# A mixture-of-experts stage whose places of 96 and 64 slots stand in another sequence

## Chip, cores and metric

One NeuronCore of a Trainium2 chip. The metric is the device time of one execution in microseconds (us). The kernel before was timed in three runs: 1676.42 us median, 1673.38 to 1678.52.

## What is computed

Two layers of an encoder over 256 tokens of width 1024, in float32. Layer 0 mixes by a recurrence and a state space model, then attends to a memory, then goes through a dense feed-forward. Layer 1 mixes by differential attention, attends to the memory, and ends in eight experts of which each token takes two. The change touches the experts alone:

```python
top_logits, top_idx = lax.top_k(logits, TOP_K)
top_w = jax.nn.softmax(top_logits, axis=-1)
gates = jnp.sum(jax.nn.one_hot(top_idx, N_EXPERTS, dtype=F32) * top_w[..., None], axis=-2)
out = jnp.zeros(h.shape, F32)
for e in range(N_EXPERTS):
    y_e = swiglu(h, w_gate[e], w_up[e], w_down[e]).astype(F32)
    out = out + gates[..., e:e + 1] * y_e
```

An expert's hidden width is 3584, so its three matrices hold 3 x 1024 x 3584 floats, 44.04 MB, and all eight 352 MB.

## The kernel before, in words

The stage of the experts is a loop over eight *places*, `r` = 0 to 7 (the last loop of the kernel, under `manual_schedule`, so TensorE's order is the order of the code). A place handles one expert, and only the tokens that chose it: these are gathered into a fixed number of slots, 96 or 64. `NG[r]` says how many groups of 32 slots place `r` has, 3 or 2; in the kernel before it is (3, 3, 2, 3, 2, 3, 3, 2). Place 0 always holds expert 0. The other seven experts are sorted by their number of tokens on the chip (`order`, L1730 on), and the table `by_size` in `_constants` hands the four with most tokens to the places of 96 and the three others to the places of 64; `caps` (L1755 to L1757) gives the capacities by that same rank, and a branch behind the loop takes up tokens that did not fit. In this data nothing overflows: the branch's body is not in the trace.

In a place, TensorE goes through four steps `i` = 0 to 3, each for two slices of 512 hidden columns (the last for two of 256):

- `up(r, i)` (L1860, its matmuls are recorded at the helper's line L195 as `pgu<-raw,gx`): the gathered tokens `gx` are the stationary operand, 32 columns at a time, the weights `raw` the moving one. Four matmuls of 32 columns lie beside each other in the array. The step has two halves of four row blocks; a half needs four pieces of weights (gate and up, of two slices), all four almost from its start.
- `hidden` and `turned` (ScalarE, VectorE, and transposes `ptA` and, with 96 slots only, `ptC`): the activation, turned for the next matmul.
- `down(r, i)` (`pd<-raw,th`), which runs one step late, behind the next `up`: four pieces of weights, the last step two.

Once a place, at fixed points of this order: `scatter` (`psc`) of the place before, twelve matmuls for 96 slots and eight for 64; `prepare(r + 1)` (`ptp`), which makes the next place's scatter matrix; and, in places 0, 2, 4 and 6 behind their last `up`, `gather` (`pgt`) for the next set of places. The sets are fixed: (0), (1, 2), (3, 4), (5, 6), (7). A gather computes as many columns for each of its places as the widest of the set has, 32 matmuls in any case.

Weights come by `piece` (L1805): a DMA of 1 MB, issued from SP's queue in the order of the code, into the next of 17 buffers in rotation (pools of 6, 2, 3, 5 and 1, L32 to L35 and L1779 to L1780). So a piece can be issued when the matmuls on the piece 17 before it are done. A place has 42 pieces: 28 for `up`, 14 for `down`. In the order of issue each place gives 8 for its first `up`, 2 for the last `down` of the place before, 8, 4, 8, 4, 4 and 4.

What the number of groups decides is in these lines of `up` and `down`: with three groups an `up` row block takes three banks of four matmuls, with two it takes two.

```python
if NG[r] == 3:
    units(p[0], [x[0], x[1], x[2], x[0]], [g0, g0, g0, g1], k == 0, k == 7)
    units(p[1], [x[0], x[1], x[2], x[0]], [u0, u0, u0, u1], k == 0, k == 7)
    units(p[2], [x[1], x[2], x[1], x[2]], [g1, g1, u1, u1], k == 0, k == 7)
else:
    units(p[0], [x[0], x[1], x[0], x[1]], [g0, g0, g1, g1], k == 0, k == 7)
    units(p[1], [x[0], x[1], x[0], x[1]], [u0, u0, u1, u1], k == 0, k == 7)
```

Of the kernel before, what the change touches and what calls it, by code (L numbers as in the profile page):

```python
# [92 lines left out]
FILL_B = 0.5  # L93
FILL_C = 16
S5_LAT = 2
NG = (3, 3, 2, 3, 2, 3, 3, 2)
GK2 = ((0, 2), (2, 4), (4, 6), (6, 8))

COLS = {}
# [24 lines left out]
def kernel(ctx: ExitStack, tc: tile.TileContext, a: dict, out: bass.AP, dbg=None):  # L124
# [1541 lines left out]
    def slots(rs, eng):  # L1666

        pf = pfp.tile([128, 2, 2, 128], F32R, name="pf", tag="pf")
        for j, r in enumerate(rs):
            how = [(pf[:, :, j], 0 if NG[r] == 3 else 2)]  # L1670
            if NG[r] == 3:
                pc = pfp.tile([128, 2, 128], F32R, name="pc", tag=f"pc{j}")
# [57 lines left out]
    def order():  # L1730
# [23 lines left out]
        v.tensor_copy(gflS[:, :, 0:9:8], gfl[:, :, 0:9:8])  # L1754
        nc.gpsimd.memset(caps, 32.0 * NG[0])  # L1755
        v.tensor_scalar(pos, pos, 3.5, -32.0, op0=ALU.is_gt, op1=ALU.mult)
# [54 lines left out]
    def gather(rs, pieces):  # L1811

        n, c = len(rs), 32 * max(NG[r] for r in rs)
        gx = gxp.tile([128, n, 8, c], F32, name="gx", tag="gx")
# [12 lines left out]
    def prepare(r):  # L1827
# [11 lines left out]
        for x, h in enumerate(hots[r]):  # L1839
# [4 lines left out]
            nc.vector.tensor_reduce(gs[:, x], gv, axis=AX.XY, op=ALU.add)  # L1844
            m = halves[:, 0:2] if NG[r] == 3 else halves[:, 2:4]
            if x == 0:
# [13 lines left out]
    def up(r, i, gather_on=None):  # L1860

        gx, n = inputs[r], 512 if i < 3 else 256
        p = [ps_mm.tile([128, 512], F32, name="pgu", tag="mm")[:, 0:n] for _ in range(NG[r])]
        for k4 in range(2):
# [354 lines left out]
```

## Time and profile before

| | us |
|---|---|
| median of three runs | 1676.42 |
| the profiled execution | 1677.01 |
| its span, first to last instruction | 1675.1 |
| TensorE busy, whole span | 1606.2 (96%) |
| mean granted clock of TensorE | 0.975 of full |
| first `up` of place 0 to the end | 799.26 to 1675.1 |

The first 800 us are everything ahead of the experts; the change does not reach them. Times below are from the start of the span. In the profile PE is TensorE, SPq the queue of SyncE that issues the DMAs, L195 the helper that records most matmuls. The trace records each float32 matmul as two, so a group of 96 in the program's order is 192 there. A busy TensorE is one whose matmuls follow each other without a wait; where it waits, the row of the matmul behind the wait shows the wait and what ended it, in square brackets.

### The profile page before, as it was taken

To read this page: it belongs to the slowest core of one execution; us is meant where nothing else is said; L and a number is where in the kernel's file an instruction comes from. 1 tells how busy PE (TensorE), PEld (TensorE's weight loads), DVE (VectorE), ACT (ScalarE), POOL (GpSimd) and SP (SyncE) were. 2 spreads that over 40 slices of the span, in tenths; PEclk is the share of its full clock that TensorE was granted. 3 is DMA by queue.
4 is the path that set the end of the run, shared out by engine and by line. 5 is a ranking of instruction groups with operands and counts; after the bars stand their busy time and mean duration, and the time that the engine had idled before them with its cause. 6 is when DMAs were issued, how large, how long until landed. Compare 5 with 4: busy or idle time off the path is not lost. (4 is left out here: it accounts for less than half of the span.)

```text
span 1675.1 us, 34301 instructions
## 1 busy us (share of the span) xinstructions
PE 1606.2 (96%) x14830; PEld 977.4 (58%) x14830; DVE 645.6 (39%) x1081; ACT 480.1 (29%) x861; POOL 207.4 (12%) x256
## 2 busy tenths in 40 slices
PE   5999999999999999998999999999999899999997
PEld 5867657899999988898324333343333323333432
DVE  7778987676555567764201011100101001011011
ACT  6465434554544456653101000010000100010000
POOL 6334473121000032111000000000000000000000
PEclk9999979999999999999899999999999999999998
DMA  6423323564555543645789889999999999999895
GB/s 224 153 89 126 105 75 113 221 257 150 181 195 173 187 147 127 251 139 201 301 354 399 335 363 405 404 419 418 418 419 418 419 419 418 418 419 392 346 419 238
DMA packets 74464, 471.50 MB, mean 281 GB/s; under 512 B 8600, under 2 KB 10008, under 8 KB 22464
## 3 DMA queue, kind: packets, MB, share of 16 engines
q1 hardware_dynamic: 73024, 465.02, 71.5%
q0 software_dynamic: 1280, 4.20, 0.7%
q8 instruction: 118, 1.93, 0.5%
q14 instruction: 42, 0.34, 0.1%
HBM read 463.94 MB, written 5.24 MB: 280 GB/s over the span
## 5 line engine op out<-in xcount | busy, mean ns | idle before, releaser
L195 PE MATMUL pgu<-raw,gx 128*32 128x512 f32 (+1 forms) x5376 | 520.5, 544 | 5.7 <-DMA raw<-mg 3.3
L195 PEld LDWEIGHTS pgu<-raw,gx 128*32 128x32 f32 x5376 | 171.4, 111 | 330.8 <-issue 290.0
L195 PE MATMUL pd<-raw,th 128*32 128x512 f32 x2352 | 262.7, 597 | 0.4 <-DVE th L1908 0.4
L184 DVE TENSOR_TENSOR wl<-raw,wh 128x1024 fp32r<-128x1024 f32 (+1 forms) x159 | 194.0, 1232 | 105.2 <-ACT wh L178 104.9
L178 ACT ACTIVATE wh<-raw 128x1024 fp32r<-128x1024 f32 (+1 forms) x160 | 165.6, 1047 | 149.2 <-PE pgu L191 69.2
L1894 DVE SCALAR_TENSOR_TENSOR actA<-pgu,gs,actA 128x512 f32<-128x512 f32 (+1 forms) x32 | 21.9, 684 | 481.2 <-ACT actA L1890 272.6
L195 PEld LDWEIGHTS pd<-raw,th 128*32 128x32 f32 x2352 | 76.4, 111 | 174.9 <-issue 171.8
L190 PE MATMUL pm<-xh,wh 128*128 128x256 f32 (+1 forms) x552 | 161.1, 295 | 15.2 <-ACT wh L178 13.3
L192 PE MATMUL pm<-xh,wl 128*128 128x256 f32 (+1 forms) x552 | 157.9, 290 | 5.3 <-DVE wl L184 5.3
L191 PE MATMUL pm<-xl,wh 128*128 128x256 f32 (+1 forms) x552 | 158.6, 289 | 2.1 <-DVE xl L1096 2.1
L1890 ACT ACTIVATE actA<-pgu,gs 128x512 f32<-128x512 f32 (+1 forms) x32 | 20.3, 635 | 444.8 <-PE pgu L195 444.7
L190 PEld LDWEIGHTS pm<-xh,wh 128*128 128x128 f32 (+1 forms) x552 | 106.7, 194 | 18.4 <-ACT wh L178 13.8
L192 PEld LDWEIGHTS pm<-xh,wl 128*128 128x128 f32 (+1 forms) x552 | 106.1, 194 | 7.4 <-DVE wl L184 6.6
L191 PEld LDWEIGHTS pm<-xl,wh 128*128 128x128 f32 (+1 forms) x552 | 107.1, 194 | 3.6 <-DVE xl L1096 2.5
L191 PE MATMUL pgu<-xl,wh 128*128 128x256 f32 x352 | 99.3, 282 | 0.0
L190 PE MATMUL pgu<-xh,wh 128*128 128x256 f32 x352 | 99.2, 282 | 0.0
L192 PE MATMUL pgu<-xh,wl 128*128 128x256 f32 x352 | 99.1, 282 | 0.0
L1833 POOL CAST mv<-cst 128x256 fp32r<-128x256 f32 x8 | 3.6, 448 | 650.9 <-PE ptp L195 626.0
L192 PEld LDWEIGHTS pgu<-xh,wl 128*128 128x128 f32 x352 | 66.4, 189 | 0.0
L191 PEld LDWEIGHTS pgu<-xl,wh 128*128 128x128 f32 x352 | 66.3, 188 | 0.0
L190 PEld LDWEIGHTS pgu<-xh,wh 128*128 128x128 f32 x352 | 66.2, 188 | 0.0
L453 DVE SCALAR_TENSOR_TENSOR fwl<-fraw,cols,fwh 128x512 fp32r<-128x512 f32 x64 | 56.1, 885 | 11.6 <-ACT fwh L450 11.6
(482 smaller groups left out, 2182.3 us busy)
## 6 DMA issues: line engine op xcount, KB each, us to landing
raw<-mg SPq DMA_DIRECT2D x112, 1024.0 KB, 19.1
raw<-mu SPq DMA_DIRECT2D x112, 1024.0 KB, 17.9
raw<-md SPq DMA_DIRECT2D x112, 1024.0 KB, 18.7
raw<-wgu SPq DMA_DIRECT2D x22, 1024.0 KB, 4.9
fraw<-wkv SPq DMA_DIRECT2D x32, 512.0 KB, 3.8
raw<-wqkv SPq DMA_DIRECT2D x12, 1024.0 KB, 4.9
raw<-wdn SPq DMA_DIRECT2D x11, 1024.0 KB, 4.8
raw<-hy SPq DMA_DIRECT2D x16, 512.0 KB, 3.9
```

The costliest lines, as they stand in the source:

```text
L178: W["act"].append(nc.scalar.activation(wh, rv, AF.Copy).ins)
L184: W["dve"].append(e_.tensor_tensor(wl[:, c_], rv[:, c_], wh[:, c_], op=ALU.subtract).ins)
L190: nc.tensor.matmul(out, lhsT=lt[0], rhs=r[0], start=start, stop=False, **kw)
L191: nc.tensor.matmul(out, lhsT=lt[0], rhs=r[1], start=False, stop=False, **kw)
L192: nc.tensor.matmul(out, lhsT=lt[1], rhs=r[0], start=False, stop=stop, **kw)
L195: nc.tensor.matmul(out, lhsT=lt, rhs=r, start=start, stop=stop, **kw)
L453: e_.scalar_tensor_tensor(wl, rv, g, wh, op0=ALU.mult, op1=ALU.subtract)
L1833: nc.gpsimd.tensor_copy(mv[:, :, 0:128], ident[:, None, :].to_broadcast([128, 2, 128]))
L1890: nc.scalar.activation(actA, p[0], AF.Silu, scale=gs[:, 0, 1:2])
L1894: nc.vector.scalar_tensor_tensor(actA, p[1], gs[:, 0, 1:2], actA, op0=ALU.mult, op1=ALU.mult)
```

## The change

```diff
-NG = (3, 3, 2, 3, 2, 3, 3, 2)
+NG = (3, 2, 3, 2, 3, 2, 3, 3)
```

One table is changed. The places go from 96, 96, 64, 96, 64, 96, 96, 64 slots to 96, 64, 96, 64, 96, 64, 96, 96. There are still five of 96 and three of 64. `by_size`, the sets' widths, the scatter and the buffers of sums follow from the table; every transfer, its size and its place in SP's queue stay as they were, and POOL's order too.

TensorE at place 1, from the last `down` of place 0's third step on. Before:

```order
L195 MATMUL pd<-raw,th 32x512 x48
L1907 MATMUL ptA<-cst,actA 128x128 x2
L1913 MATMUL ptC<-cst,actC 128x64 x2
L195 MATMUL pgu<-raw,gx 32x512 x96
L195 MATMUL pd<-raw,th 32x512 x24
L1907 MATMUL ptA<-cst,actA 128x128 x4
L1913 MATMUL ptC<-cst,actC 128x64 x4
L195 MATMUL pgu<-raw,gx 32x512 x96
L195 MATMUL pd<-raw,th 32x512 x48
```

And now:

```order
L195 MATMUL pd<-raw,th 32x512 x48
L1907 MATMUL ptA<-cst,actA 128x128 x2
L1913 MATMUL ptC<-cst,actC 128x64 x2
L195 MATMUL pgu<-raw,gx 32x512 x64
L195 MATMUL pd<-raw,th 32x512 x24
L1907 MATMUL ptA<-cst,actA 128x128 x4
L195 MATMUL pgu<-raw,gx 32x512 x64
L195 MATMUL pd<-raw,th 32x512 x32
```

Place 1's `up` steps have 64 matmuls instead of 96 on the same eight pieces of weights, and its transposes of `actC` are gone; they stand in place 2 now.

TensorE at the end of place 7, from its third `up` on. Before:

```order
L195 MATMUL pgu<-raw,gx 32x512 x64
L195 MATMUL pd<-raw,th 32x512 x32
L1907 MATMUL ptA<-cst,actA 128x128 x4
L195 MATMUL pgu<-raw,gx 32x256 x64
L195 MATMUL pd<-raw,th 32x512 x32
L1907 MATMUL ptA<-cst,actA 128x128 x2
L195 MATMUL pd<-raw,th 32x512 x16
L195 MATMUL psc<-yh,pTs 128x512
```

And now:

```order
L195 MATMUL pgu<-raw,gx 32x512 x96
L195 MATMUL pd<-raw,th 32x512 x48
L1907 MATMUL ptA<-cst,actA 128x128 x4
L1913 MATMUL ptC<-cst,actC 128x64 x4
L195 MATMUL pgu<-raw,gx 32x256 x96
L195 MATMUL pd<-raw,th 32x512 x48
L1907 MATMUL ptA<-cst,actA 128x128 x2
L1913 MATMUL ptC<-cst,actC 128x64 x2
L195 MATMUL pd<-raw,th 32x512 x24
L195 MATMUL psc<-yh,pTs 128x512
```

The last place has 96 slots, so each of its groups is half as long again, and twelve `psc` follow instead of eight.

TensorE at the end of place 6, the gather for place 7 (the first two and the last of 32 rows that repeat). Before:

```order
L195 MATMUL pgu<-raw,gx 32x256 x96
L195 MATMUL pgt<-pf,hnh 128x64
L195 MATMUL pgt<-pf,hnl 128x64
...
L195 MATMUL pgt<-pf,hnl 128x64
L195 MATMUL pd<-raw,th 32x512 x48
```

And now:

```order
L195 MATMUL pgu<-raw,gx 32x256 x96
L195 MATMUL pgt<-pf,hnh 128x96
L195 MATMUL pgt<-pf,hnl 128x96
...
L195 MATMUL pgt<-pf,hnl 128x96
L195 MATMUL pd<-raw,th 32x512 x48
```

The gather keeps its 32 matmuls, and each is 32 columns wider. The other three gathers are 192 columns wide before and now.

## Rows read from the trace of the kernel before

**Rows 1.** Windows, places 1 to 7: length, engines' busy time, PEclk, DMA share, GB/s.
```profile
922.57:1040.83 118.26, 115.94 (x1148) 40.42 (x1147) 13.07 (x25) 9.06 (x19) 0.73 (x3) 1.00 0.91 365
1040.83:1126.22 85.39, 84.26 (x816) 31.65 (x815) 9.53 (x19) 8.18 (x17) 0.73 (x3) 1.00 1.00 411
1126.22:1241.99 115.77, 113.46 (x1128) 39.08 (x1127) 12.55 (x24) 8.26 (x17) 0.73 (x3) 1.00 1.01 419
1241.99:1330.29 88.30, 85.50 (x817) 31.82 (x815) 8.96 (x17) 8.18 (x17) 0.73 (x3) 1.00 1.01 418
1330.29:1454.08 123.79, 117.97 (x1130) 39.30 (x1129) 12.26 (x23) 8.53 (x18) 0.81 (x3) 0.97 1.01 419
1454.08:1578.69 124.61, 123.02 (x1181) 44.81 (x1179) 12.10 (x21) 10.17 (x23) 0.00 (x0) 0.97 0.98 400
1578.69:1662.85 84.16, 83.42 (x812) 28.51 (x810) 8.43 (x15) 5.74 (x12) 0.00 (x0) 1.00 0.87 356
```

**Rows 2.** Waits of TensorE for weights, 840 to 1675: total us, times, longest.
```profile
PE pgu L195 <- DMA raw<-mg: 3.3, 1, 3.3
PE pgu L195 <- DMA raw<-mu: 2.5, 3, 0.9
```

**Rows 3.** The chain that ended last, at place 5: start, us, what.
```profile
1316.08 21.00 DMA raw<-mu
...
1337.13 21.78 PE pgu L195 x177
```

**Rows 4.** Timeline of TensorE, first up step of places 1 and 2: start, us.
```profile
922.57 20.81 PE L195 MATMUL pgu<-raw,gx 128*32 128x512 f32 x192
...
1040.83 13.94 PE L195 MATMUL pgu<-raw,gx 128*32 128x512 f32 x128
```

**Rows 5.** Timeline of SP's queue at the start of place 1.
```profile
922.06 0.33 SPq L1808 DMA_DIRECT2D raw<-mg  x1
931.40 0.33 SPq L1808 DMA_DIRECT2D raw<-mu  x1
```

**Rows 6.** Tile raw, the one DMA issued from 931.3 to 931.8.
```profile
DMA to landing us min/median/max: 5.0/5.0/5.0
```

**Rows 7.** Timeline of SP's queue, the last down pieces of places 2 and 4.
```profile
1222.26 0.33 SPq L1808 DMA_DIRECT2D raw<-md  x1
...
1434.83 0.33 SPq L1808 DMA_DIRECT2D raw<-md  x1
```

**Rows 8.** Timeline of TensorE, the gather in place 2, first row and the row behind.
```profile
1115.10 0.36 PE L195 MATMUL pgt<-pf,hnh 128*128 128x192 f32 x1
...
1118.85 7.07 PE L195 MATMUL pd<-raw,th 128*32 128x512 f32 x64
```

**Rows 9.** Window of 1 us behind the wait of place 5, columns as in rows 1.
```profile
1335.00:1336.00 1.00, 1.00 (x8) 0.00 (x0) 0.00 (x0) 0.00 (x0) 0.00 (x0) 0.50 1.03 426
```

**Rows 10.** Timeline of TensorE in place 1, preparing place 2.
```profile
1016.30 0.44 PE L195 MATMUL ptp<-mv,pf 128*128 128x132 f32 x2
1016.58 0.62 PE L1907 MATMUL ptA<-cst,actA 128*128 128x128 f32 x4
1019.01 0.46 PE L1913 MATMUL ptC<-cst,actC 64*128 64x64 f32 x4 [1.81 <-ACT th L1909]
```

**Rows 11.** The chain in place 6: the last two down pieces of place 5.
```profile
1474.88 5.15 PE pd L195 x48
```

**Rows 12.** Timeline of TensorE at the end, two matmuls of the last scatter.
```profile
1664.74 0.39 PE L195 MATMUL psc<-yh,pTs 128*128 128x512 f32 x1
1664.97 0.40 PE L195 MATMUL psc<-yl,pTs 128*128 128x512 f32 x1
```

**Rows 13.** The gather in place 6: timeline of TensorE, and a window's row (columns as in rows 1).
```profile
1560.62 0.30 PE L195 MATMUL pgt<-pf,hnh 128*128 128x64 f32 x1
...
1564.87 13.25 PE L195 MATMUL pd<-raw,th 128*32 128x512 f32 x96
...
1569.00:1570.00 1.00, 1.00 (x9) 0.20 (x5) 0.00 (x0) 0.00 (x0) 0.00 (x0) 0.50 0.45 188
```

## The prediction

> **What bounds the kernel now.** I read the windows first, one for each expert place from the first of its up matmuls to the first of the next place's [rows 1]. The reader is to see two things in them. A place of 96 slots holds TensorE for 115.8 to 124.6 us, one of 64 for 84.2 to 88.3, and TensorE is busy in nearly all of it. Beside that the transfers run at 418 to 419 GB/s in places 3 to 5 but at 365 in place 1 and 400 in place 6. Each place brings in the same 42 pieces of 1 MB, 44.04 MB, so a place of 96 is slower than its weights and a place of 64 faster. Which of the two is late changes from place to place: where transfers fall below 419 GB/s the 17 piece buffers are full and the transfers wait for TensorE; where TensorE waits, the buffers are empty.
>
> Then the waits: TensorE waits for a weight transfer only 3.3 and 2.5 us in all [rows 2]. The chain of waits shows where: a transfer of mu issued at 1316.08 lands at 1337.09 and releases the up matmuls of place 5 [rows 3]. From 1337.09 to the end the chain holds no transfer, so it is TensorE's own work. So the time is: the landing of the fourth piece of the last place that starved (place 5), plus TensorE's work after it. I price the change by the same two numbers.
>
> **The change.** SP's order, and so the order and the sizes of the transfers, is the same row for row. TensorE's matmuls are the same in number, except that the last gather is 32 columns wider; the work of places 1 and 2, 3 and 4, 5 and 6 is exchanged in part so that 96 and 64 alternate up to place 6, and the last place holds 96 instead of 64. Five places still hold 96, and the capacities are still given by an expert's rank in size (four largest, and expert 0), so the branch for overfull places is entered neither more nor less. Slots, scatter and the POOL copies move with their places; those on DVE, ACT and POOL run beside TensorE's 20.8 us up steps, so they cost nothing.
>
> *Step 1, when transfers run freely.* Up to 922.57 only the preparation for place 1 differs, by less than 1 us. There the buffers are full: SP issues a piece at 922.06 and the next only at 931.40 [rows 5], when place 1 has let go of its first piece. An up step of 96 takes 20.81 us, of 64 13.94 [rows 4], half of it 10.40 or 6.97. Before, the buffer came free 1.57 us ahead of the end of the half (922.57 + 10.40 - 931.40); scaled to 64 that is 1.05, so the piece goes out at 922.57 + 6.97 - 1.05 = 928.5. It lands 5.0 us later as before [rows 6]: 933.5. After it, place 1 frees four pieces in 6.97 us, faster than they arrive, so the full buffers should not stop the transfers again before place 7. Place 1 of the kernel before went on stopping them: that is its 365 GB/s.
>
> *Step 2, when place 6 can start.* The piece of step 1 is the last of the second up step of place 1. The fourth piece of place 6 is the 196th after it (five places of 42, less 14). With the transfers running freely, the same two pieces of down weights come round after 212.57 us for two places (1222.26 to 1434.83) [rows 7]: 106.3 a place, 2.531 a piece, 414 GB/s with the small gaps in it. The windows agree within 1% with 419 [rows 1]. The Trainium skill (DMA: Bandwidth & Descriptors, Where 436 GB/s comes from) puts the ceiling of the sixteen ports higher, at 435 GB/s; by that figure a place would take 101.2 us and the end would come out as in rival A below. I take the row. 196 x 2.531 = 496.1, so place 6 has its first weights at 1429.6.
>
> *Step 3, does TensorE wait for them?* A 64 after a 96 takes 85.39 (place 2) [rows 1], less its gather of 3.75 (1115.10 to 1118.85) [rows 8], which now lies in the places of 96: 81.6. A 96 after a 64 takes 115.77 (place 3) [rows 1] plus that gather: 119.5. A pair is 201.1 us of TensorE against 212.6 of transfers, so each pair must lose about 11.5 us to waits once the lead is gone. Place 1 ends at 922.6 + 81.6 = 1004.2, and the fourth piece of place 2 lands at 933.5 + 28 x 2.531 = 1004.4: the lead is just used up. Place 2 ends at 1123.9 and place 3 at 1205.5, the fourth piece of place 4 lands at 933.5 + 112 x 2.531 = 1217.0: a wait of 11.5. Place 4 and 5 end at about 1419.9 (a clock fall in place 4, below, shortens only the next wait), place 6 starts at 1429.6: a wait of 9.7. So some 21 us of waits stand where 5.8 stood, and step 2 sets the time.
>
> *Step 4, from there to the end.* From the landing of its fourth piece (1337.09) place 5, a 96 after a 64 and ahead of a 96, took until 1454.08 [rows 1, 3]: 117.0. This holds the price of the half clock behind the wait [rows 9]. Place 6 is the same with a gather, 117.0 + 3.75 = 120.7, and ends at 1550.3. Place 7 is a 96 after a 96, as place 1 was: 118.26 [rows 1], less 2.1 for preparing a further place (its ptp from 1016.30 to 1016.58 and the 1.81 ahead of ptC) [rows 10], plus its last two down pieces 5.15 [rows 11]: 121.3. The last down matmul ends at 1671.6, before it ended at 1662.85 (place 7) [rows 1].
>
> *Step 5, the tail.* Behind it came 12.25 us of scaling, scatter and store (1662.85 to 1675.1). A 96 scatters with twelve matmuls instead of eight; the scaling of its second sum is done beside the first scatter matmuls. Four more at 0.23 [rows 12]: 0.9. The span ends at 1671.6 + 13.15 = 1684.8, 9.7 later. The profiled execution took 1677.0, 1.9 more than its span, and lies 0.6 above the median 1676.4: forecast **1686.7**, taken as 1687.
>
> **What is unknown.** The last gather now moves 96 columns. With 64 columns the granted clock fell to 0.50 (1.2 of 2.4 GHz) in its course, and the 96 down matmuls behind it took 13.25 us [rows 13], against twice 5.15 for as many at full clock [rows 11]; in places 2 and 4, with gathers of 192, it stood at 1.00 throughout [rows 1]. So the fall costs 0 or 2.9; two of these three gathers had none, so I take 0 and keep 2.9. The waits are longer than before, so more of the work behind them may run at half clock: in place 5 it cost 1.0 us (the first up step took 21.78 from the landing on, 20.81 at full clock [rows 3, 4]), behind the gather 2.9; so up to 1.9 more. The cadence: 44.04 MB at 419 GB/s is 105.1 us, which over 196 pieces is 5.6 sooner; a short stop of the transfers in place 2, as the 411 GB/s there [rows 1], is 1.6 later.
>
> **The rivals.** *A, TensorE stays the bound and the order is free (faster).* If weights were never late, the end would be 922.6 + 3 x 81.6 + 2 x 119.5 + 119.5 + 121.3 = 1647.2 for the last down, 1660.4 with the tail, 1662.3 in all, 14.7 less. It decides at the start of place 6: 1406.4 without waits, so 196 pieces in 472.9 us, 101.3 a place, 434.7 GB/s. No place shows over 419 [rows 1], not even places 3 and 4, where free buffers stood ready throughout: chance 0.05. The ceiling of 435 GB/s of the Trainium skill (DMA: Bandwidth & Descriptors, Where 436 GB/s comes from) would just allow it; this trace stays 4% below. *B, no change.* The waits are there, but with the cadence at 105.1 a place: 1686.7 - 5.6 = 1681.1, or 1680.1 if there is no half clock behind the last wait. For it speaks that one place of the trace moved at full 419; against it, that rows 7 hold the 106.3 over two. Chance 0.14. *C, slower still.* The gather's fall (2.9) and up to 1.9 us more at half clock add: 1689.6 to 1691.5; a fall in place 4 is swallowed by the wait before place 6, one in place 6 or 7 by nothing. Chance 0.26. That the change does nothing is excluded by the order on TensorE.
>
> **How the numbers follow.** The forecast's own case (1682 to 1689.5) has 0.55. The range 1680 to 1697 takes in B, and at its upper end C with two further stops of the transfers like that of place 2; it leaves out A and what lies beyond either end, some 0.15 in all. A measurement can tell 0.3% here, 5.0 us: faster is A (0.05), within is B (0.14), slower the rest (0.81).
>
> **What would show it.** Right: place 1 at 80 to 84 us with 390 GB/s or more; the second wait of SP ending near 928.5; waits for mg and mu of about 10 us each at the starts of places 4 and 6, a clock of 0.50 behind them, near none at place 7; the fourth piece of place 6 landing near 1430; the last weights issued earlier than before, though the span ends later. Wrong: no waits at place 6 (A), or the landing near 1424 (B); a half clock behind the last gather is C. If the span is longer but place 6 starts by 1430, steps 4 and 5 are mis-sized; if it starts late, step 1 or 2.

## The result, and the profile after

The change is slower: 1686.05 us median of five runs (1685.04 to 1688.07) against 1673.73 for the kernel before (five runs, 1672.96 to 1678.52). The ratio is 1.0067, 95% interval 1.0051 to 1.0083. The forecast was 1687. The medians lie 12.3 us apart, by the ratio it is 11.2. The profiled execution after took 1685.04, the shortest of the five, and its span is 1683.1.

The windows of the kernel after, one for each place from 1 to 7, with the columns of [rows 1]:

```profile
922.19:1006.05 83.86, 82.13 (x784) 28.80 (x782) 10.43 (x23) 6.32 (x13) 0.73 (x3) 0.98 0.97 398
1006.05:1124.92 118.87, 117.35 (x1160) 42.64 (x1159) 11.60 (x20) 10.23 (x21) 0.73 (x3) 1.00 1.01 419
1124.92:1209.56 84.64, 81.33 (x784) 28.93 (x782) 10.57 (x24) 6.31 (x13) 0.73 (x3) 1.00 1.01 418
1209.56:1336.08 126.52, 120.50 (x1158) 42.43 (x1158) 11.44 (x20) 10.22 (x21) 0.73 (x3) 0.97 1.01 419
1336.08:1422.27 86.19, 82.32 (x784) 28.06 (x783) 9.69 (x20) 6.31 (x13) 0.73 (x3) 1.00 1.01 418
1422.27:1549.98 127.71, 121.81 (x1160) 42.85 (x1160) 11.46 (x20) 9.75 (x22) 0.00 (x0) 0.97 1.01 418
1549.98:1671.73 121.75, 120.99 (x1195) 41.69 (x1193) 11.72 (x20) 9.56 (x21) 0.00 (x0) 1.00 0.69 280
```

Place 1 moves 398 GB/s where it moved 365, and places 2 to 6 all stand at 418 or 419, the most that any place shows: from place 2 to place 6 the transfers are stopped no more. Places 4 and 6 hold TensorE 126.5 and 127.7 us, 11 to 12 longer than the 115.8 of place 3 before [rows 1]. Of that 3.75 is their gather, the rest waits and half clock. Only in place 7 do the transfers fall, to 280: the last piece lands at 1640.0, and in the 31.7 us that TensorE then still needs for its matmuls up to 1671.7 hardly anything is moved (2 GB/s).

SP's queue at the start of place 1, after, which answers to [rows 5]:

```profile
921.69 0.33 SPq L1808 DMA_DIRECT2D raw<-mg  x1
928.44 0.33 SPq L1808 DMA_DIRECT2D raw<-mu  x1
```

The stop ends at 928.44 instead of 931.40. The chain of waits, after, around the start of place 6 (start, us, what), which answers to [rows 3]:

```profile
1389.64 19.96 DMA raw<-mu
...
1409.72 19.86 DMA raw<-mu
...
1429.62 21.77 PE pgu L195 x177
```

The fourth piece of place 6 lands just ahead of 1429.62, and from there the chain holds no transfer any more: it is TensorE, with short steps of VectorE and ScalarE between its matmuls. Before, this handover stood at place 5, at 1337.13, with a 96, a 96 and a 64 to go; now it stands at place 6 with two of 96 to go. TensorE's waits for weights, 840 to the end (total us, times, longest), which answer to [rows 2]:

```profile
PEld pgu L195 <- DMA raw<-mg: 10.9, 5, 4.8
PEld pgu L195 <- DMA raw<-mu: 8.5, 8, 2.3
PE pgu L195 <- DMA raw<-mg: 8.3, 4, 3.9
PEld pd L195 <- DMA raw<-md: 4.7, 4, 1.4
PE pgu L195 <- DMA raw<-mu: 2.4, 5, 0.8
PE pd L195 <- DMA raw<-md: 2.3, 4, 0.7
```

The matmuls waited 13.0 us where they had waited 5.8. The rows of PEld, TensorE's loads of the stationary operand, which the trace records by themselves, give about twice as much, 24.1 in the three largest. The same rows of the kernel before:

```profile
PEld pgu L195 <- DMA raw<-mu: 5.7, 4, 2.3
PEld pgu L195 <- DMA raw<-mg: 4.8, 3, 4.2
```

10.5 us there. Which of the two, matmuls or weight loads, comes nearer to the loss is taken up below, with the lighter transfers.

### The profile page after: what moved, and what is told of

Read it like the earlier page. It is cut to its first block, busy times and chain, and to the rows that moved or that the text cites. A ratio compares the mean times of both kernels' runs of the same rounds, so it can differ in the third digit from the quotient of the medians.

```text
span 1683.1 us, 34300 instructions
## 1 busy us (share of the span) xinstructions
PE 1608.1 (96%) x14830; PEld 975.4 (58%) x14830; DVE 645.3 (38%) x1081; ACT 480.2 (29%) x861; POOL 207.2 (12%) x256
## 4 chain that ended last, share of the span: by engine, by line
PE 77%; DMA 10%; DVE 8%; POOL 2%; ACT 2%; issue 1%; SPq 0%; DVEq 0%; POOLq 0%; ACTq 0%
PE pgu L195 27%; PE pd L195 12%; DMA raw<-mu 7%; PE pm L190 5%; PE pm L191 5%; PE pm L192 5%; PE pgu L190 2%; PE pgu L191 2%; PE pgu L192 2%; DMA raw<-md 2%; PE pm L195 2%; PE pf L190 2%; PE pf L191 1%; PE pf L192 1%; PE po L195 1%
## 5 line engine op out<-in xcount | busy, mean ns | idle before, releaser
L195 PE MATMUL pgu<-raw,gx 128*32 128x512 f32 (+1 forms) x5376 | 527.1, 549 | 10.7 <-DMA raw<-mg 8.3
```

The costliest lines, as they stand in the source:

```text
L195: nc.tensor.matmul(out, lhsT=lt, rhs=r, start=start, stop=stop, **kw)
```

## The experiments

The theory is the prediction's ledger: the time is the landing of the weights of the last place that starved, plus TensorE's work after it; if no place starves, TensorE's own sum. Two rivals were set against it. *Last place*: what costs is only that place 7 now holds 96, since its work stands uncovered at the end. *Alternation*: each change of size between neighbours costs TensorE time of its own (preparation, widths of gathers, clock).

### Another sequence with one early 64

```diff
-NG = (3, 3, 2, 3, 2, 3, 3, 2)
+NG = (3, 2, 3, 3, 2, 3, 3, 2)
```

> Sequence 96, 64, 96, 96, 64, 96, 96, 64. Ledger theory (the time is the landing of the weights of the last place that starved, or TensorE's own sum if none does, plus TensorE's work after it): a 64 at place 1 ends the stops of the transfers early, as in the change, and no two pairs of 96 and 64 follow that would use up the lead; 1006 + 119.5 + 117 + 85.4 = 1328 at place 5, whose fourth piece lands at 1323, so TensorE never waits more than 2 us in all; end of the span near 1328 + 115.8 + 121 + 84.2 + 12.3 = 1661, time 1663, 8 to 13 below the kernel before. Rival 'last place' (what costs is that place 7 holds 96): it ends on 64, so it is as the kernel before, within 3 us. Rival 'alternation' (every change of size between neighbours costs TensorE time of its own): as many changes as the kernel before, so no gain.

Measured: 1663.7 us median of six against 1672.72 for the kernel before (17 runs), ratio 0.9946 (0.9933 to 0.9959): 9.0 faster than before. The change is 12.3 slower than before, so some 21 us lie between the two sequences, each taken against the kernel before as it was timed beside it. Its windows, places 1 to 7:

```profile
922.15:1004.33 82.18, 80.45 (x784) 28.11 (x783) 10.43 (x23) 6.33 (x13) 0.73 (x3) 1.00 0.97 398
1004.33:1123.35 119.02, 117.70 (x1162) 42.91 (x1161) 12.30 (x23) 10.41 (x22) 0.72 (x3) 1.00 1.01 418
1123.35:1241.61 118.26, 115.86 (x1148) 40.42 (x1146) 13.05 (x25) 9.08 (x19) 0.72 (x3) 1.00 1.00 411
1241.61:1327.02 85.41, 84.28 (x817) 31.66 (x815) 8.95 (x17) 8.20 (x17) 0.73 (x3) 1.00 1.01 415
1327.02:1442.57 115.55, 113.81 (x1130) 39.36 (x1129) 12.26 (x23) 8.56 (x18) 0.81 (x3) 1.00 1.01 419
1442.57:1565.56 122.99, 121.40 (x1180) 44.30 (x1178) 12.10 (x21) 10.20 (x23) 0.00 (x0) 0.99 1.00 408
1565.56:1649.68 84.12, 83.42 (x812) 28.52 (x810) 8.43 (x15) 5.75 (x12) 0.00 (x0) 1.00 0.87 357
```

The transfers are stopped little before place 7 (411 GB/s in place 3, 408 in place 6) and TensorE almost never waits: no matmul in its list of waits stands behind a weight transfer, and the weight loads wait 3.5 us for them in all. The two places of 96 at 2 and 3 let the lead grow again before the 64 at place 4 uses it. There are five places of 96 and three of 64 as in the change, and only the last gather is narrower: the sequence is worth some 21 us between the two. Both rivals, which saw no gain here, fail.

### A sequence that ends on 96 without starving early

```diff
-NG = (3, 3, 2, 3, 2, 3, 3, 2)
+NG = (3, 2, 3, 3, 2, 3, 2, 3)
```

> Sequence 96, 64, 96, 96, 64, 96, 64, 96. Ends on a 96 as the change does. Ledger theory: nothing starves before place 7; its fourth piece lands at 933.5 + 238 x 2.531 = 1536, place 6 ends near 1525, a wait of about 10 there, then 1536 + 122 + 12 = 1670 of span: within 3 us of the kernel before. Rival 'last place': as the change, 10 to 13 us above the kernel before. Rival 'alternation': one change more than the kernel before, 2 us or more above it.

Measured: 1670.3 us median of ten against 1672.72, ratio 0.998 (0.9971 to 0.9989). Its chain at place 7:

```profile
1520.88 19.93 DMA raw<-mu
...
1540.86 21.12 PE pgu L195 x177
```

The last place holds 96, as in the change, and the time is that of the kernel before, even a little less. So *last place* does not explain the 12.3 us of the change. A cost there is all the same: from the sequence with one early 64 this one differs only in that places 6 and 7 are exchanged, and it takes 6.6 us more (1670.3 against 1663.7). Its weight loads waited for mg and mu, 3.5 us in place 6 and 5.4 at the start of place 7, where the other sequence's waited 3.5 for weights in all. What a 96 at the end costs without such waits is shown below with lighter transfers. The wait at place 7 was smaller than the 10 expected (3.6 by the matmuls), because place 6 ended at 1535 instead of 1525 and the weights landed 5 later. Part of that belongs to the profiled execution, the longest of the ten (1674.61): up to the end of place 5 its order is that of the sequence with one early 64, yet its place 4 begins 4.2 us later (1245.82 against 1241.61), and place 3, where the buffers were full for a time, ran at 404 GB/s instead of 411.

### A sequence that ends on 64 and starves

```diff
-NG = (3, 3, 2, 3, 2, 3, 3, 2)
+NG = (3, 3, 3, 2, 3, 2, 3, 2)
```

> Sequence 96, 96, 96, 64, 96, 64, 96, 64. Ends on a 64 as the kernel before does. Ledger theory: three places of 96 with full buffers stop the transfers for about 12 us more than before, then the pairs starve TensorE twice, about 19 us of waits in all; 7 to 12 us above the kernel before. Rival 'last place': as the kernel before, within 3 us.

Measured: 1680.67 us median of four against 1672.72, ratio 1.0049 (1.0034 to 1.0063), 8 above. Its windows of places 1, 2, 6 and 7:

```profile
921.41:1039.88 118.47, 116.37 (x1150) 40.70 (x1148) 13.78 (x28) 9.36 (x20) 0.80 (x3) 1.00 0.92 366
1039.88:1161.23 121.35, 119.77 (x1181) 43.98 (x1179) 12.10 (x21) 11.05 (x23) 0.73 (x3) 1.00 0.93 372
...
1448.93:1576.05 127.12, 121.20 (x1158) 42.54 (x1159) 11.35 (x20) 9.38 (x21) 0.00 (x0) 0.97 1.01 419
1576.05:1665.92 89.87, 85.42 (x812) 30.37 (x810) 8.42 (x15) 5.75 (x12) 0.00 (x0) 1.00 0.94 388
```

Here the loss is on both sides: two places with stopped transfers (366 and 372 GB/s) and, later, places 6 and 7 that wait for weights (127.1 and 89.9 us). It ends on 64 and is slower all the same; *last place* expected no difference. Its chain holds a transfer to the very end, the last piece of down weights:

```profile
1643.98 19.87 DMA raw<-md
...
1663.99 1.96 PE pd L195 x16
```

So the landing that counts is not always the fourth piece of a place. Place 7 had its first weights in time (its fourth piece landed at 1562.6, it began at 1576.05) and ran out of them on the way, because a 64 takes less time (84 us) than its 42 pieces need (106).

### The same two sequences with lighter transfers

Half of every piece of down weights is not loaded; the loaded half is used for both. The down product is another one, the matmuls keep their number and size.

```diff
-        nc.sync.dma_start(t, src[:, lo:hi])
+        nc.sync.dma_start(t[:, 0:hi - lo], src[:, lo:hi])
...
-                w = piece(source("md", r, s), 2048 * k2, 2048 * k2 + 2048).rearrange("p (k h n) -> p k h n", k=2, h=2)
+                w = piece(source("md", r, s), 2048 * k2, 2048 * k2 + 1024)[:, 0:1024].rearrange("p (h n) -> p h n", h=2)
```

with `w[:, k, h]` and `w[:, k, 1]` read as `w[:, h]` and `w[:, 1]`. For the sequence of the kernel before:

> The sequence of the kernel before, with half of every piece of down weights not loaded (the first half is used twice, so the down product is another one); TensorE's matmuls are the same in number and size. A place brings in 35 MB instead of 42, at 2.5 us a piece 88 to 89 us, less than a 96 or a mean place takes on TensorE. Ledger theory: TensorE never waits and its own sum is left: a span near 1661, time 8 to 13 us below the kernel before. Rival 'alternation' or 'last place': the time stays within 6 us of the kernel before, since only the waits of 5.8 us go.

For the sequence of the change:

> The sequence of the change with the same halved down weights. Ledger theory: with the transfers out of the way the sequence is free; within 3 us of the sequence of the kernel before with halved weights, that is about 20 us below the change itself. Rival 'last place' or 'alternation': it stays 8 us or more above the old sequence with halved weights.

Measured: 1662.7 us (old sequence, four runs) and 1660.82 (new, four runs), against 1674.81 for the kernel before: ratios 0.9935 (0.9916 to 0.9953) and 0.9926 (0.9906 to 0.9945). The new sequence loses its whole disadvantage, 12.3 us, and stands 1.9 below the old one, with intervals that overlap. Against the change it is 25 us less, more than the 20 expected. Windows of the new sequence with light transfers, places 1 to 7:

```profile
920.73:1004.60 83.87, 82.14 (x785) 28.81 (x783) 10.43 (x23) 6.32 (x13) 0.73 (x3) 0.98 0.97 386
1004.60:1123.46 118.86, 117.34 (x1159) 42.62 (x1159) 11.59 (x20) 10.23 (x21) 0.73 (x3) 1.00 0.90 347
1123.46:1205.58 82.12, 80.39 (x785) 28.11 (x783) 10.43 (x23) 6.32 (x13) 0.73 (x3) 1.00 0.97 386
1205.58:1324.44 118.86, 117.34 (x1160) 42.62 (x1159) 11.60 (x20) 10.22 (x21) 0.73 (x3) 1.00 0.90 351
1324.44:1406.28 81.84, 80.36 (x784) 28.10 (x782) 9.40 (x19) 6.31 (x13) 0.73 (x3) 1.00 0.97 389
1406.28:1525.24 118.96, 117.64 (x1161) 42.90 (x1160) 11.76 (x21) 9.75 (x22) 0.00 (x0) 1.00 0.90 354
1525.24:1647.00 121.76, 121.00 (x1195) 41.70 (x1193) 11.73 (x20) 9.56 (x21) 0.00 (x0) 1.00 0.50 186
```

This is what the prediction's rival A describes, with its condition met by lighter weights instead of a faster path: place 6 starts at 1406.28 (1406.4 in its sum) and the last down matmul ends at 1647.0 (1647.2). That the two agree to 0.2 us is partly chance: place 1 began 1.9 us earlier than in the sum and took 2.3 more. The new sequence ends on 96 and is not slower than the old one, which ends on 64, so a 96 at the end costs nothing where the weights are in time. *Alternation* fails: without late weights the alternating sequence costs TensorE nothing.

Place by place against the windows of the change, this run also says what late weights cost there: 2.5 us in place 3, 7.7 in place 4, 4.4 in place 5 and 8.8 in place 6, in places 1, 2 and 7 nothing; 23.3 in all. The same for the kernel before: the old sequence with light transfers, places 4 and 5:

```profile
1242.04:1327.43 85.39, 84.25 (x816) 31.65 (x815) 8.95 (x17) 8.17 (x17) 0.73 (x3) 1.00 1.01 404
1327.43:1442.97 115.54, 113.80 (x1129) 39.36 (x1128) 12.25 (x23) 8.52 (x18) 0.81 (x3) 1.00 0.88 343
```

88.30 and 123.79 stood there [rows 1], so late weights cost 2.9 + 8.3 = 11.2 us. Both sums lie near the waits of the weight loads (24.1 and 10.5), not near those of the matmuls (13.0 and 5.8). They hold the half clock behind the waits too, which is no wait, so the nearness is an observation of these two kernels and not a law.

### Two buffers fewer

```diff
-RAW5 = 5
+RAW5 = 3
```

For the kernel before:

> The kernel before with 15 buffers for pieces instead of 17. Ledger theory: the lead that the full buffers hold is two pieces, 5.1 us, shorter where the stops end, so weights land about 5 us later from then on and every us of it is waited for: 4 to 7 us above the kernel before. If the lead did not matter: no change.

For the change:

> The change with 15 buffers for pieces instead of 17. Ledger theory: the last stop is at the start of place 1 and then the transfers run freely, so all landings, the one of place 6 too, are two pieces later: 5 us (4 to 6) above the change, the fourth piece of place 6 at about 1434.6 instead of 1429.6. If the waits at places 4 and 6 had nothing to do with what the buffers held at place 1: no change.

Measured: 1680.62 us (ten runs) for the old sequence against 1674.81, ratio 1.0028 (1.0013 to 1.0044), which is 4.7 us (5.8 by the medians); 1692.29 (four runs) for the new, ratio 1.0101 (1.0078 to 1.0124), 5.7 us above the 1.0067 of the change (6.2 by the medians). The chain of the old sequence with 15 buffers, at place 5:

```profile
1340.76 21.87 PE pgu L195 x177
```

The fourth piece landed at 1340.71, 545.1 us behind the first gather matmul of the stage (795.58); in the kernel before it was 539.7 (797.41 to 1337.09). That is 5.4 later, two pieces. The chain of the new sequence with 15 buffers, at place 6:

```profile
1418.34 19.84 DMA raw<-mu
...
1438.21 20.72 PE pgu L195 x177
```

The handover is at the same place, at 1438.2. In this execution the whole stage began 4.8 us later: its first gather matmul at 800.31, in the change at 795.47. Counted from there the landing is 3.75 us later, a little less than the five of two pieces. So the times agree with the theory, and the profile of the old sequence agrees in size, that of the new in place and sign; that the whole 5.7 us of the new is the lead is not shown, since a later start of the stage lies in the one execution that was profiled.

## Why the prediction was right

**Step 1** gave 928.5 for the end of the stop; it was 928.44. **Step 2** gave 1429.6 for the weights of place 6; TensorE was released at 1429.62. The cadence of 2.531 us a piece, taken over two places of the kernel before, held over 196 pieces. (The two pieces of [rows 7] are the last down pieces of places 3 and 5, not 2 and 4; they stand two places apart all the same.) That the deciding number came out to a tenth of a us is in part luck: place 1 began 0.4 us earlier than in the sum (922.19), and its first buffer came free 0.7 us ahead of the end of the half instead of 1.05, which nearly cancels. The mechanism is not luck: the same sum gives 1004.4 and 1217.0 for the fourth pieces of places 2 and 4, and they landed at 1004.6 and 1217.0.

**Step 3** forecast 21 us of waits at the starts of places 4 and 6 (11.5 and 9.7). Against the run with light transfers late weights cost 10.2 us at places 3 and 4 and 13.1 at 5 and 6, 23.3 in all, half clock included: right in size. The place is right only in part, since 6.9 of it lies ahead, in places 3 and 5. At the starts of places 4 and 6 themselves the weight loads waited 7.6 us each for mg and mu and the matmuls 4.7 and 4.9, where about 10 each had been named as the sign; the granted clock behind both was 0.50 (at 1217 and at 1430), and place 7 had near none of these waits, as forecast. (The 1419.9 for the end of place 5 does not follow from the terms shown, which give 1418.1, or 1419.3 with step 4's 120.7; it was 1422.27.) What step 3 also had wrong is the number it compared with: 5.8 us before, read from the matmuls' waits, where the loss was 11.2. So the change adds 12 us of loss, not 15. The number did not enter the sum, which goes by the landing. And it missed that TensorE is slow in place 1, 83.86 us instead of 81.6: its last up step ran at half clock in part, and the preparation waited longer than in the place it was priced from. Of the two the clock is the larger: with one early 64 the same place stood at 1.00 and took 82.18. Timeline of TensorE in place 1, after, and a window in it:

```profile
989.50 0.66 PE L1907 MATMUL ptA<-cst,actA 128*128 128x128 f32 x4 [1.42 <-ACT pTs L1850]
990.09 8.80 PE L195 MATMUL pgu<-raw,gx 128*32 128x256 f32 x128
```

```profile
992.00:993.00 1.00, 1.00 (x16) 0.51 (x12) 0.00 (x0) 0.00 (x0) 0.00 (x0) 0.50 1.07 442
```

The result did not move for it, for the reason that step 2 gave: a place that waits for its weights starts when they land, whatever TensorE lost before. Errors ahead of the last wait are swallowed by it.

**Step 4** forecast 120.7 us from the landing to the end of place 6, measured 120.4 (1429.6 to 1549.98), and 121.3 for place 7, measured 121.75. The last down matmul ended at 1671.73, forecast 1671.6. **Step 5** was 1.7 too long: 13.15 us for the tail, 11.4 measured (1671.73 to 1683.1). TensorE and ScalarE at the end, after:

```profile
1670.94 0.69 ACT L1942 ACTIVATE yh<-pd,gs 128x512 fp32r<-128x512 f32 x1 [4.26 <-PE pd L195]
...
1675.42 0.39 PE L195 MATMUL psc<-yh,pTs 128*128 128x512 f32 x1
...
1675.65 0.39 PE L195 MATMUL psc<-yl,pTs 128*128 128x512 f32 x1
```

With two sums, the first is complete before the last down matmuls, so its scaling starts at 1670.94, 0.8 us ahead of their end; with one sum it could only start behind them. The last scatter matmuls follow each other at 0.23 us. Of the kernel before step 5 read two at 0.23 [rows 12], but its last four took twice that; the granted clock fell to 0.50 behind the first of these:

```profile
1665.68 1.84 PE psc L195 x4
```

Of the 1.7, some 0.5 us lies behind the last addition (6.9 us from there to the end before, 6.3 now). The forecast is counted from the profiled execution of before (1677.0 and 9.7 more); the 0.6 by which it names that one above the median is not taken off. The profiled execution after lies 1.0 below the median of its five, and the tail was 1.7 too long. These pull in opposite ways, so that the forecast lies 1 us from the median is partly luck.

**The unknowns.** The fall of the clock behind the last gather (C) did not come. The 96 down matmuls behind it took the 10.4 us of full clock, not 13.25 [rows 13]:

```profile
1538.98 10.44 PE pd L195 x96
```

The price of half clock behind a wait was misread. The prediction puts it at 1.0 us, 21.78 us against 20.81; but the 21.78 are 177 matmuls [rows 3] and the 20.81 are 192 [rows 4]. At that pace 177 take 19.2, so it was 2.6, and the "up to 1.9 more" was not there to come: the same 177 took 21.77 after. The sum is not touched, because step 4 takes place 5 whole.

The measured difference, 12.3 us, is larger than the forecast's 10.3 against the median shown then, 1676.4; with two more runs the kernel before has its median at 1673.73, and the profiled execution, from which all was counted, took 1677.0. Its fall of the clock in place 6 is 2.9 of these 3.3 us. Its mean granted clock was 0.975, and of the 30 later executions of the kernel before the eight at 0.975 or 0.976 took 1675.3 to 1678.4 us, the 22 at 0.977 or more 1671.7 to 1675.2. That the fall explains the difference is likely from this; where the clock fell in those executions is not shown.

**What is shown and what is argued.** Shown by runs: the sequence is free when weights are light; a 96 at the end is not by itself the cost; a 64 at the end is no cure; with two buffers fewer, and so a shorter lead, the weights land later and the time is longer. Argued is how the 23.3 us divide into waits and half clock. In plain words: the fourth piece of place 5 landed at 1323.3, one place's transfers ahead of 1429.6 and 13.8 us earlier than the 1337.1 of before. The change gained that in the main at place 1, where the transfers are stopped less. It could not use it: each pair of 96 and 64 needs 11.5 us less of TensorE than of transfers, so TensorE ran into the landings at places 4 and 6, and two places of 96, 242 us, were left where a 96, a 96 and a 64 of 326 us had been with the handover 92.5 us earlier.

## To carry to other kernels

Where two resources take turns at being late, a share of busy time says little; keep a ledger of the lead, place by place, and find the last place that starves: the time is its landing plus the work after it. Order the pieces of work so that the buffered lead is neither full (the transfers stop) nor empty (the engine stops): here 96, 64, 96, 96, 64, 96, 96, 64 gave 1663.7 us, 9 less than before, by a table of eight numbers. A heavy piece at the end is not dear by itself: with its weights in time it cost nothing here. It is dear where the last wait stands shortly ahead of it, because all of its work then follows that wait.

## What the runs showed of the hardware that was not expected

The granted clock falls at some places in some executions only. Behind or in the last gather of 64 columns, place 6 stood at 0.97 in the kernel before and, with 15 buffers, again, but at 1.00 with light transfers; of five profiles with a gather of 64 there, two show the fall in full, one in part (0.99) and two not. The windows of place 6, of the kernel before with 15 buffers and of the old sequence with light transfers:

```profile
1457.81:1582.40 124.59, 123.01 (x1181) 44.72 (x1179) 12.10 (x21) 10.17 (x23) 0.00 (x0) 0.97 0.96 386
```

```profile
1442.97:1564.28 121.31, 119.71 (x1181) 43.98 (x1179) 12.12 (x21) 10.16 (x23) 0.00 (x0) 1.00 0.82 311
```

The two differ by 3.3 us, about the price that the prediction kept for it. With 96 columns it came once as well: behind the last gather of the new sequence with 15 buffers a window shows 0.50, where the change shows none.

```profile
1547.00:1548.00 1.00, 1.00 (x8) 0.21 (x4) 0.00 (x0) 0.00 (x0) 0.00 (x0) 0.50 1.01 418
```

So a forecast that is counted from one profiled execution carries some 3 us that belong to that execution. And in both kernels the waits of TensorE's weight loads came near to what late weights cost against the light runs, while those of its matmuls showed about half of it.
